# Eight zero products at the head, x^T by token halves, and the last LayerNorms dealt out anew in a two-layer decoder trunk

## The chip, the cores and the metric

The kernel runs on one core of one Trainium2 chip, in one launch. The metric is the device time of that launch in microseconds (us); lower is better. Five engines work side by side and meet through semaphores: TensorE (PE in the profile; its weight loads stand apart as PEld), VectorE (DVE), ScalarE (ACT), GpSimd (POOL) and SyncE (SP), whose part here is to issue DMAs.

## The reference

Two layers (DEPTH = 2) over 1024 tokens of width 1024 in float32. Layer 0 mixes tokens with a gated DeltaNet, layer 1 with a complex diagonal state-space layer (S5); each runs beside a 4-head cross-attention into 256 memory tokens. Cut to what matters:

```
for i in range(2):
    if i == 0:  mix, xq = gdn_mixer(x, ...)    # q, k, v, z, beta, g from one projection of x;
                                               # short conv, chunked delta rule, 8 heads
    else:       mix, xq = s5_mixer(x, ...)
    cross = memory_attention(xq, mem, w_kv[i])
    x = layer_norm(ALPHA * x + concat(mix, cross) @ w_o[i], ln1_g[i], ln1_b[i])
    x = layer_norm(ALPHA * x + square(relu(x @ w1[i])) @ w2[i], ln2_g[i], ln2_b[i])
```

`layer_norm` takes mean and variance over the 1024 channels of a token, and multiplies by (variance + 1e-5)^-1/2, a gain and a bias.

## The kernel before, in words

**Products.** Every float32 operand is split in two parts, high = the value rounded to the type fp32r (a copy on ACT) and low = the rest (a subtraction on DVE), and a product is three matmuls, high x high, high x low and low x high (`mm3`, L397 to L399). Activations are held transposed, channels on the 128 partitions and tokens in two halves of 512 (`HALF`), so a matmul has 512 columns and a projection of one block of 128 outputs takes 8 channel blocks k (`KT`) x 3 matmuls for each half.

**The first stage.** `load_xT` loads the first weight block (tile `wir`, 512 KB, split into `wih` and `wil` by `load_split`, L354, L363 and L364), the 16 gate columns (`wba`, 64 KB), then the eight 512 KB blocks of x^T (tile `x`, L981 and L983). L993 and L994 split x into `xTh` and `xTl`. Two jobs on PE eat these: `ba` (L1011 and L1012, gate columns, two matmuls for a block and half) and `wi` (first key projection, three matmuls). `gdn_consts` fills constants before that.

**The recurrence stage.** From about 205 to 695 us the delta rule runs head by head. Its chain, for each pair of 64-token chunks, is: `ks` on PE, R on DVE (L1431), `pe` on PE (L1435), a copy `e` on ACT (L1437), `pS` and `po` on PE (L1441, L1447), the new state S on DVE (L1446). Projections of the next head (`wi`, `wz`) fill PE between. DVE also works, four times, on the inverse of a triangular matrix (tile X, L1233 and L1235, 16 instructions in a row). L1335 (`mix`) and L1329 (`gb`) prepare a chunk for this chain.

**The end.** `mlp_last` computes the last two matrices of the second MLP: for each block tau of 128 tokens two PE groups (tile `tm`, 12 matmuls each), each added onto y by DVE (L938), and after a block's second group `done` calls `layer_norm`. That has two forms. In the DVE form bn_stats, bn_aggr, a scale and shift of the variance (L509 to L511) are DVE's; in the `junk` form ACT takes the sums and the squares (L502, L505) with three one-column steps on DVE between. In both forms POOL raises to the power -1/2 (L512), and DVE makes two passes over the row (L522 and L523; L514 and L517 for the last block, whose second pass and store are cut in two). In layer 1 blocks 5 and 6 take the ACT form.

**What sets the order.** The program is written in one order, and at the end `settle` reorders all of it, from `self.begin` on: it takes the written order of PE as due times, goes through a list schedule with a price for every instruction (`price`), an input being ready at `r + length + lag`, and fixes the order that results on each engine. Every engine then runs its own list strictly in order. A change of one price or of one rule can therefore move instructions far from the lines that were edited.

Of the kernel before, what the change touches and what calls it, by code (L numbers as in the profile page):

```python
# [10 lines left out]
F32 = mybir.dt.float32  # L11
F32R = mybir.dt.float32r
AF = mybir.ActivationFunctionType
ALU = mybir.AluOpType
# [15 lines left out]
def f32(ap):  # L30
    return ap.bitcast(F32)


class Trunk:
# [27 lines left out]
    def settle(self, first, last, reach=0.0, ahead=15.0, passes=1, margin=0.0, late=0.0, hold=1e3):  # L62
# [118 lines left out]
        for _ in range(passes):  # L181
# [36 lines left out]
            while len(order) < n:  # L218
# [48 lines left out]
                for y in after[x] + then[x]:  # L267
                    same = e == E.PE and ins[y].engine == e
                    ready[y] = max(ready[y], r + (0.0 if x not in deps[y] else busy if same else length + lag + (margin if ins[y].engine == E.PE else 0.0)))
# [222 lines left out]

    def layer_norm(self, y, gb, junk=None, last=None):
# [4 lines left out]
        mv = self.tile("st", [P, 4], F32, "mv")  # L498
        if junk is not None:
            s = st.rearrange("p a b -> p (a b)")  # L500
            for c in range(2):
                nc.scalar.activation(junk, halves[c], AF.Copy, accum_out=s[:, c:c + 1])  # L502
            nc.vector.tensor_scalar(mv[:, 0:1], s[:, 0:1], s[:, 1:2], -1.0 / 1024, op0=ALU.add, op1=ALU.mult)
            for c in range(2):
                nc.scalar.activation(junk, halves[c], AF.Square, bias=mv[:, 0:1], accum_out=s[:, 4 + c:5 + c])  # L505
            nc.vector.scalar_tensor_tensor(mv[:, 2:3], s[:, 4:5], s[:, 5:6], self.eps_ln, op0=ALU.add, op1=ALU.add)
        else:
            for c in range(2):
                nc.vector.bn_stats(st[:, c, :], halves[c])  # L509
            nc.vector.bn_aggr(mv[:, 0:2], st)  # L510
            nc.vector.tensor_scalar(mv[:, 2:3], mv[:, 1:2], 1024.0, 1024 * 1e-5, op0=ALU.mult, op1=ALU.add)  # L511
        nc.gpsimd.tensor_tensor(mv[:, 3:4], mv[:, 2:3], self.mhalf[:, 0:1], op=ALU.pow)  # L512
        if last is not None:
            nc.vector.scalar_tensor_tensor(y, y, mv[:, 0:1], gb[0], op0=ALU.subtract, op1=ALU.mult)  # L514
            for c in range(2):
                c = slice(c * HALF, (c + 1) * HALF)
                nc.vector.scalar_tensor_tensor(y[:, c], y[:, c], mv[:, 3:4], gb[1][:, c], op0=ALU.mult, op1=ALU.add)  # L517
                nc.sync.dma_start(last[:, c], y[:, c])
            return
        parts = [(y, slice(0, 1024))] if not isinstance(y, list) else [(y[c], slice(c * HALF, (c + 1) * HALF)) for c in range(2)]  # L520
        for o, c in parts:
            nc.vector.scalar_tensor_tensor(o, o, mv[:, 0:1], gb[0][:, c], op0=ALU.subtract if junk is None else ALU.add, op1=ALU.mult)  # L522
            nc.vector.scalar_tensor_tensor(o, o, mv[:, 3:4], gb[1][:, c], op0=ALU.mult, op1=ALU.add)  # L523
# [417 lines left out]


    def gdn_consts(self):
        nc = self.nc
# [26 lines left out]
    def load_xT(self, wba):  # L971

        nc = self.nc
        w0 = self.load_split(self.a["w_in"][8], "w1", "wi")
        nc.sync.dma_start(wba, self.a["wba"])
        self.begin = nc.cur_bb.bb.instructions[-1]
        raw = self.quad(F32, "x") + self.quad(F32, "x")
        for k in range(KT):
            if k == 0:
                for h in range(2):  # L980
                    nc.sync.dma_start(raw[0][:, h * HALF:(h + 1) * HALF], self.a["xT"][0:P, h * HALF:(h + 1) * HALF])  # L981
                continue
            nc.sync.dma_start(raw[k], self.a["xT"][k * P:(k + 1) * P])  # L983
# [4 lines left out]
        xT = self.new_xT()  # L988
        for k in range(KT):
            for h in range(2):  # L990
                s = raw[k][:, h * HALF:(h + 1) * HALF]
                hi, lo = xT[h][0][:, k, :], xT[h][1][:, k, :]
                nc.scalar.copy(hi, s)  # L993
                nc.vector.tensor_tensor(lo, s, f32(hi), op=ALU.subtract)  # L994
        return xT, w0
# [1212 lines left out]
    def run(self):  # L2208
# [131 lines left out]
    def mlp_block(self, i, B, ahead, xd, side, out, more):  # L2340
        new = []

        def done(y, tau):
            if tau == 0:
                self.gb2 = self.load_gb(self.a["ln2_g"][i:i + 1], self.a["ln2_b"][i:i + 1])
                self.nc.scalar.activation(self.gb2[0], self.gb2[0], AF.Copy, scale=32.0)
                if more:
                    new.extend(self.new_xT())
            self.layer_norm(y[tau], self.gb2, self.psum("mm", "jk") if tau in ((), (5, 6))[i] else None, last=out[tau] if tau == 7 and not more else None)
            if tau < 7 or more:  # L2350
# [96 lines left out]
```

## Time and profile before

| | us |
|---|---|
| median of 3 runs | 2511.4 (2509.89, 2511.4, 2513.75) |
| the profiled execution | 2512.02 |
| its span, first to last instruction | 2510.3 |
| PE busy in the span | 2471.1 (98%) |
| DVE busy | 1969.6 (78%) |
| ACT busy | 1283.0 (51%) |
| POOL busy | 435.9 (17%) |

DMA moves 481 MB, 192 GB/s on the mean. The mean granted TensorE clock is 0.998. PE works nearly all the time, so what counts is where it does not: the span less PE's busy time is 39 us, which the table of stretches puts at 7.9 us in the first 50, 10 us after 2490, 8.8 us between 400 and 600, and the rest in small pieces. In the profile, the column in brackets behind a row is the time for which the engine stood idle before it and what ended that.

### The profile page before, as it was taken

Reading aid. Unit: us, or ns where it says so; the run is one execution under the profiler, and the core shown is the slowest. Engines: PE = TensorE matmul, PEld = TensorE weight load, DVE = VectorE, ACT = ScalarE, POOL = GpSimd, SP = SyncE. Lnnn points to the kernel's source line nnn. Section 1 sums busy time; section 2 is a strip of 40 time slices with the busy share of each in tenths; the row PEclk is TensorE's granted clock in tenths of the full one; section 3 lists DMA queues with packets and bytes.
Section 4 is the critical chain, followed back from the end, with each engine's and each line's share of the span. In section 5 each row is a group of like instructions: output and inputs, shape, how many; then the busy total and the mean of one; then the engine's idle time right before and its main releaser. Section 6 shows DMA issues by size and latency. Waiting matters only on the chain.

```text
span 2510.3 us, 36952 instructions
## 1 busy us (share of the span) xinstructions
PE 2471.1 (98%) x12181; PEld 2063.9 (82%) x12181; DVE 1969.6 (78%) x3676; ACT 1283.0 (51%) x2730; POOL 435.9 (17%) x673
## 2 busy tenths in 40 slices
PE   8999999999999999999999999999999999999998
PEld 6888887887887887888888888888887888888886
DVE  7786888777779798879988957786687666578788
ACT  6665555554556576554444244564365555544441
POOL 1232332414002023212210123112011000000000
PEclk9999999999999999999999999999999999999999
DMA  6464585767854567487454489669736434574532
GB/s 211 119 163 125 138 257 135 237 189 226 270 166 157 192 218 236 154 297 240 148 161 134 157 245 301 214 216 331 259 131 206 155 143 164 216 255 133 168 105 97
DMA packets 320769, 481.17 MB, mean 192 GB/s; under 512 B 110225, under 2 KB 141153, under 8 KB 320577
## 3 DMA queue, kind: packets, MB, share of 16 engines
q1 hardware_dynamic: 293056, 423.76, 51.9%
q0 software_dynamic: 25216, 50.86, 6.9%
q10 hardware_dynamic: 2304, 4.20, 0.4%
q8 instruction: 96, 1.57, 0.3%
q14 instruction: 97, 0.79, 0.1%
HBM read 321.91 MB, written 156.73 MB: 191 GB/s over the span
## 4 chain that ended last, share of the span: by engine, by line
PE 87%; DVE 5%; ACT 3%; DMA 2%; issue 2%; POOL 1%; SPq 0%; DVEq 0%; POOLq 0%; ACTq 0%
PE q L398 7%; PE q L397 7%; PE q L399 7%; PE tm L397 4%; PE tm L399 4%; PE tm L398 4%; PE pA L399 3%; PE pA L397 3%; PE pA L398 3%; PE wi L397 3%; PE wi L399 3%; PE wi L398 3%; PE pC L399 2%; PE pC L397 2%; PE pC L398 2%; PE pB L397 2%
## 5 line engine op out<-in xcount | busy, mean ns | idle before, releaser
L397 PE MATMUL q<-wkh,hkh 128*128 128x512 f32 x784 | 306.2, 391 | 0.7 <-ACT G L1886 0.7
L398 PE MATMUL q<-wkl,hkh 128*128 128x512 f32 x784 | 305.9, 390 | 0.5 <-DVE wkl L901 0.5
L399 PE MATMUL q<-wkh,hkl 128*128 128x512 f32 x784 | 305.4, 390 | 0.0
L900 ACT CAST wkh<-wr 128x512 fp32r<-128x512 f32 x168 | 104.9, 624 | 237.5 <-PE q L398 186.2
L512 POOL TENSOR_TENSOR mv<-mv,mhalf 128x1 f32<-128x1 f32 x32 | 26.7, 833 | 858.9 <-DVE mv L511 634.6
L397 PEld LDWEIGHTS q<-wkh,hkh 128*128 128x128 f32 x784 | 147.2, 188 | 32.2 <-ACT G L1886 1.6
L398 PEld LDWEIGHTS q<-wkl,hkh 128*128 128x128 f32 x784 | 147.3, 188 | 31.0 <-DVE wkl L901 1.1
L399 PEld LDWEIGHTS q<-wkh,hkl 128*128 128x128 f32 x784 | 147.2, 188 | 30.5
L901 DVE TENSOR_TENSOR wkl<-wr,wkh 128x512 fp32r<-128x512 f32 x168 | 115.5, 688 | 65.8 <-issue 55.6
L397 PE MATMUL wi<-xTh,wih 128*128 128x512 f32 x384 | 159.9, 416 | 0.2 <-ACT qT L1098 0.2
L398 PE MATMUL wi<-xTl,wih 128*128 128x512 f32 x384 | 152.6, 397 | 0.0
L399 PE MATMUL wi<-xTh,wil 128*128 128x512 f32 x384 | 152.4, 397 | 0.0
L901 DVE TENSOR_TENSOR hkl<-hr,hkh 128x512 fp32r<-128x512 f32 x196 | 133.9, 683 | 0.2 <-ACT hkh L900 0.2
L900 ACT CAST hkh<-hr 128x512 fp32r<-128x512 f32 x196 | 120.8, 616 | 1.3 <-DMA hr<-hd 1.2
L397 PE MATMUL tm<-so 128*128 128x512 f32 x280 | 109.8, 397 | 0.0
L1621 ACT CAST so<-or 128x1024 fp32r<-128x1024 f32 x70 | 72.0, 1049 | 59.5 <-DMA or<-wod 42.0
L1622 DVE TENSOR_TENSOR so<-or,so 128x1024 fp32r<-128x1024 f32 x70 | 84.5, 1220 | 16.1 <-ACT so L1621 16.0
L398 PE MATMUL tm<-so 128*128 128x512 f32 x224 | 88.2, 394 | 0.0
L399 PE MATMUL tm<-so 128*128 128x512 f32 x224 | 87.4, 391 | 0.0
L399 PEld LDWEIGHTS wi<-xTh,wil 128*128 128x128 f32 x384 | 72.7, 189 | 14.8
L397 PEld LDWEIGHTS wi<-xTh,wih 128*128 128x128 f32 x384 | 73.2, 191 | 12.5 <-ACT qT L1098 0.6
L398 PEld LDWEIGHTS wi<-xTl,wih 128*128 128x128 f32 x384 | 73.2, 191 | 11.6 <-issue 0.3
(588 smaller groups left out, 7381.8 us busy)
## 6 DMA issues: line engine op xcount, KB each, us to landing
hr<-hd SPq DMA_DIRECT2D x212, 256.0 KB, 2.8
wr<-in_w_dram SPq DMA_DIRECT2D x56, 512.0 KB, 5.0
hd<-u SPq DMA_DIRECT2D x92, 256.0 KB, 2.0
w1r<-in_w_dram SPq DMA_DIRECT2D x32, 512.0 KB, 3.5
hd<-hid SPq DMA_DIRECT2D x60, 256.0 KB, 2.3
hd<-p SPq DMA_DIRECT2D x60, 256.0 KB, 2.2
w1r<-in_w_dram SPq DMA_DIRECT2D x56, 256.0 KB, 3.6
wir<-in_w_in_dram SPq DMA_DIRECT2D x24, 512.0 KB, 3.9
```

Source lines behind the costliest of these rows:

```text
L397: mm(ps, a[0], b[0], start=start, stop=False, skip_group_check=onto)
L398: mm(ps, a[0], b[1], start=False, stop=False, skip_group_check=onto)
L399: mm(ps, a[1], b[0], start=False, stop=stop, skip_group_check=onto)
L512: nc.gpsimd.tensor_tensor(mv[:, 3:4], mv[:, 2:3], self.mhalf[:, 0:1], op=ALU.pow)
L900: nc.scalar.copy(hi, s)
L901: nc.vector.tensor_tensor(lo, s, f32(hi), op=ALU.subtract)
L1621: nc.scalar.copy(hi, r)
L1622: V.tensor_tensor(lo, r, f32(hi), op=ALU.subtract)
```

## The change

It has three parts, and a fourth that follows from them.

1. **The head.** `rouse(8)` puts eight products of a zero tile with itself (128x128, float32) at PE's head; nothing reads them. `load_xT` now issues a half piece of x^T (256 KB: block 0, first 512 tokens) ahead of all, then the gate columns, then the first weight block, then all first halves of x^T, then all second halves. The first weight block is split in two steps of 512 columns.
2. **The last LayerNorms** (`end=True`, layer 1 only). The variance is no longer scaled by 1024: one DVE addition of (0, 1e-5) onto (mean, variance) takes the place of the scale and shift, and both passes wait for its result; the gain is not multiplied by 32 on ACT. Blocks 2, 3 and 4 take the ACT form in place of 5 and 6.
3. **A rule of `settle`.** For instructions written in the last 60 us of the program that are no DMA, an input from the same engine counts as ready at `busy + 0.06` in place of `length + lag`.
4. **The order.** `settle` runs over all of the changed program, and the order comes out differently in the first 60 us, in the recurrence stage, in parts of the first MLP and at the end.

```diff
-                    same = e == E.PE and ins[y].engine == e
-                    ready[y] = max(ready[y], r + (0.0 if x not in deps[y] else busy if same else length + lag + ...))
+                    same = ins[y].engine == e and (e == E.PE or not moves and spot[x] > now - 60.0)
+                    ready[y] = max(ready[y], r + (0.0 if x not in deps[y] else busy + (0.0 if e == E.PE else 0.06) if same else length + lag + ...))
...
+        elif end:
+            for c in range(2):
+                nc.vector.bn_stats(st[:, c, :], halves[c])
+            nc.vector.bn_aggr(mv[:, 4:6], st)
+            nc.vector.tensor_tensor(mv[:, 1:3], mv[:, 4:6], self.eps2, op=ALU.add)
...
+    def rouse(self, n):
+        z = self.tile("h2", [P, P], F32, "z")
+        self.nc.vector.memset(z, 0.0)
+        ps = self.psum("mm", "z", (P, P))
+        for k in range(n):
+            self.nc.tensor.matmul(ps, z, z, start=True, stop=True)
...
-        w0 = self.load_split(self.a["w_in"][8], "w1", "wi")
+        raw = self.quad(F32, "x") + self.quad(F32, "x")
+        nc.sync.dma_start(raw[0][:, 0:HALF], self.a["xT"][0:P, 0:HALF])
         nc.sync.dma_start(wba, self.a["wba"])
+        r0 = self.load_raw(self.a["w_in"][8], "wir")
...
+        for h in range(2):
+            for k in range(KT):
+                if k or h:
+                    nc.sync.dma_start(raw[k][:, h * HALF:(h + 1) * HALF], self.a["xT"][k * P:(k + 1) * P, h * HALF:(h + 1) * HALF])
...
+        self.rouse(8)
         self.gdn_consts()
...
-            self.layer_norm(y[tau], self.gb2, self.psum("mm", "jk") if tau in ((), (5, 6))[i] else None, ...)
+            self.layer_norm(y[tau], self.gb2, self.psum("mm", "jk") if tau in ((), (2, 3, 4))[i] else None, ..., end=not more)
```

**Place one, the head of the program.** SP's list before (`wir` is the weight block, `x_110` holds blocks 0 to 3 of x^T and `x_111` blocks 4 to 7):

```order
L354 DMA wir_103<-in_w_in_dram 128x1024
L975 DMA wba_102<-in_wba_dram 128x128
L981 DMA x_110<-in_xT_dram 128x512
L983 DMA x_111<-in_xT_dram 128x1024
L983 DMA x_110<-in_xT_dram 128x1024 x3
L983 DMA x_111<-in_xT_dram 128x1024 x3
```

and now (`x_114` and `x_115` are the two holders; L1056 is a 4 KB load for the gates):

```order
L992 DMA x_114<-in_xT_dram 128x512
L993 DMA wba_113<-in_wba_dram 128x128
L354 DMA wir_118<-in_w_in_dram 128x1024
L1013 DMA x_114<-in_xT_dram 128x512 x3
L1013 DMA x_115<-in_xT_dram 128x512 x3
L1056 DMA scr_90<-in_dtb_dram 128x8
L1013 DMA x_115<-in_xT_dram 128x512
```

The weight block has gone from first to third, and every piece of x^T behind it is half as large. PE's list now begins with the zero products, and both gate products of block 0 stand ahead of the first one that needs the weight block:

```order
L958 MATMUL z_81<-z_79 128x128 x8
L1038 MATMUL ba_186<-xTh_9_120,wbah_181 32x512
L1039 MATMUL ba_186<-xTl_10_121,wbah_181 16x512
L397 MATMUL wi_292<-xTh_9_120,wih_126 128x512
L398 MATMUL wi_292<-xTl_10_121,wih_126 128x512
L399 MATMUL wi_292<-xTh_9_120,wil_127 128x512
```

Before, the first five products were L1011, L397, L1012, L398 and L399.

**Place two, DVE in the recurrence stage, at the inverse that ran from 563 to 574 us.** Before (the rows on X that are left out by ending the piece here are 14 more of L1233 and L1235):

```order
L1431 SCALAR_TENSOR_TENSOR R_6176<-ks_6174,scr_79,mix_1733 128x128
L1100 SCALAR_TENSOR_TENSOR vT_6056<-cv_6057,scr_79,vT_6056 128x512 x2
L1446 SCALAR_TENSOR_TENSOR S_6234<-S_6150,scr_79,pS_6232 128x128
L1100 SCALAR_TENSOR_TENSOR vT_6056<-cv_6057,scr_79,vT_6056 128x512
L364 TENSOR_TENSOR wil_6471<-wir_6468,wih_6470 128x1024
L1233 TENSOR_TENSOR pr_5538<-X_946_5531,st_950_5577 128x512
L1233 TENSOR_TENSOR pr_951_5578<-X_946_5531,st_950_5577 128x512
```

Now (L1458 is R, L1362 is `mix`, L1356 is `gb`, L1260 the inverse):

```order
L1458 SCALAR_TENSOR_TENSOR R_6196<-ks_6194,scr_90,mix_1753 128x128
L1362 TENSOR_TENSOR mix_1753<-qk_6148,Dq_6142 128x512
L1127 SCALAR_TENSOR_TENSOR vT_6076<-cv_6077,scr_90,vT_6076 128x512
L1356 TENSOR_TENSOR gb_6144<-gb_6144,qT_5967 128x512
L1127 SCALAR_TENSOR_TENSOR vT_6076<-cv_6077,scr_90,vT_6076 128x512
L1473 SCALAR_TENSOR_TENSOR S_6254<-S_6170,scr_90,pS_6252 128x128
L1127 SCALAR_TENSOR_TENSOR vT_6076<-cv_6077,scr_90,vT_6076 128x512
L1260 TENSOR_TENSOR pr_5558<-X_948_5551,st_952_5597 128x512
```

`mix` and `gb` have moved from behind the inverse to ahead of it, and the weight split L364 from ahead of it to behind it, and behind the next R as well.

**Place three, DVE's last rows.** Before (`tm` is a PE group, `bn` and `mv` the statistics, `y_21712` the blocks 4 to 7):

```order
L522 SCALAR_TENSOR_TENSOR y_21712<-y_21712,mv_24285,gb_24047 128x1024
L938 TENSOR_TENSOR y_21712<-tm_24310,y_21712 128x512
L523 SCALAR_TENSOR_TENSOR y_21712<-y_21712,mv_24285,gb_24049 128x1024
L509 BN_STATS bn_24324<-y_21712 128x6
L510 BN_AGGR mv_24325<-bn_24324 128x2
L514 SCALAR_TENSOR_TENSOR y_21712<-y_21712,mv_24325,gb_24047 128x1024
L511 TENSOR_SCALAR mv_24325<-mv_24325 128x1
L517 SCALAR_TENSOR_TENSOR y_21712<-y_21712,mv_24325,gb_24049 128x512 x2
```

Now (L948 adds a group, L515 is the addition of (0, 1e-5), L532 and L533 the two passes, L524 and L527 those of the last block):

```order
L532 SCALAR_TENSOR_TENSOR y_21732<-y_21732,mv_24315,gb_24067 128x1024
L948 TENSOR_TENSOR y_21732<-tm_24324,y_21732 128x512
L513 BN_STATS bn_24352<-y_21732 128x6
L533 SCALAR_TENSOR_TENSOR y_21732<-y_21732,mv_24315,gb_24069 128x1024
L948 TENSOR_TENSOR y_21732<-tm_24338,y_21732 128x512
L513 BN_STATS bn_24352<-y_21732 128x6
L514 BN_AGGR mv_24353<-bn_24352 128x2
L515 TENSOR_TENSOR mv_24353<-mv_24353,eps_24071 128x2
L524 SCALAR_TENSOR_TENSOR y_21732<-y_21732,mv_24353,gb_24067 128x1024
L527 SCALAR_TENSOR_TENSOR y_21732<-y_21732,mv_24353,gb_24069 128x512 x2
```

Both passes of block 6 now stand ahead of the last addition, and the one-column step stands ahead of the last block's first pass. From the addition of block 5's second group to that of the last one, the new list has four additions, four bn_stats, two each of bn_aggr and L515, and five passes (second of block 4, both of blocks 5 and 6).

More of the change, by code (lines that the diff above doesn't have):

```diff
@@ L491, in load_gb, with layer_norm @@
         return out
-    def layer_norm(self, y, gb, junk=None, last=None):
+    def layer_norm(self, y, gb, junk=None, last=None, end=False):
         nc = self.nc
@@ L2345, in done @@
                 self.gb2 = self.load_gb(self.a["ln2_g"][i:i + 1], self.a["ln2_b"][i:i + 1])
-                self.nc.scalar.activation(self.gb2[0], self.gb2[0], AF.Copy, scale=32.0)
+                if more:
+                    self.nc.scalar.activation(self.gb2[0], self.gb2[0], AF.Copy, scale=32.0)
+                else:
+                    self.eps2 = self.tile("st", [P, 2], F32, "eps")
+                    self.nc.gpsimd.memset(self.eps2[:, 0:1], 0.0)
+                    self.nc.gpsimd.memset(self.eps2[:, 1:2], 1e-5)
                 if more:
                     new.extend(self.new_xT())
-            self.layer_norm(y[tau], self.gb2, self.psum("mm", "jk") if tau in ((), (5, 6))[i] else None, last=out[tau] if tau == 7 and not more else None)
+            self.layer_norm(y[tau], self.gb2, self.psum("mm", "jk") if tau in ((), (2, 3, 4))[i] else None, last=out[tau] if tau == 7 and not more else None, end=not more)
             if tau < 7 or more:
```

41 lines of the change are left out of this document (24 added, 17 removed).

## The prediction

> **What bounds the kernel now.** I read the page first, then the waits of PE, then the two ends in order of time.
>
> ```profile
> PE 2471.1 (98%) x12181; PEld 2063.9 (82%) x12181; DVE 1969.6 (78%) x3676; ACT 1283.0 (51%) x2730; POOL 435.9 (17%) x673
> ...
> PE 87%; DVE 5%; ACT 3%; DMA 2%; issue 2%; POOL 1%; SPq 0%; DVEq 0%; POOLq 0%; ACTq 0%
> ```
>
> ```profile
> PE ba L1011 <- ACT xTh L993: 7.9, 2, 7.2
> PE po L1432 <- ACT on L1460: 4.3, 5, 2.4
> PE pe L1435 <- DVE R L1431: 3.0, 1, 3.0
> ```
>
> PE sets the time; 2510.3 - 2471.1 = 39 us is all that it does not work. The waits (us in total, times, longest) put 7.9 us of that on the first piece of x, and the next largest on the recurrence. So the change can only win at the head, in a few stalls, and behind PE's last product. The head, in order of time:
>
> ```profile
> 0.80 0.40 SPq L354 DMA_DIRECT2D wir<-in_w_in_dram  x1
> 0.87 0.09 DVE L1091 MEMSET cv<- 128x3 f32 x2 [0.87 <-PEq L2436]
> ...
> 1.71 0.43 SPq L981 DMA_DIRECT2D x<-in_xT_dram  x1
> ...
> 4.30 1.04 ACT L363 CAST wih<-wir 128x1024 fp32r<-128x1024 f32 x1 [2.22 <-DMA wir<-in_w_in_dram]
> 5.25 0.29 ACT L1004 CAST wbah<-wba 128x128 fp32r<-128x128 f32 x1
> ...
> 6.51 0.62 ACT L993 CAST xTh<-x 128x512 fp32r<-128x512 f32 x1 [0.96 <-DMA x<-in_xT_dram]
> ...
> 7.18 0.63 PE L1011 MATMUL ba<-xTh,wbah 128*32 128x512 f32 x1 [7.18 <-ACT xTh L993]
> ...
> 7.61 0.63 PE L397 MATMUL wi<-xTh,wih 128*128 128x512 f32 x1
> ...
> 8.30 0.62 ACT L993 CAST xTh<-x 128x512 fp32r<-128x512 f32 x1 [1.17 <-DMA x<-in_xT_dram]
> ...
> 9.54 0.62 ACT L993 CAST xTh<-x 128x512 fp32r<-128x512 f32 x1 [0.62 <-DMA x<-in_xT_dram]
> ...
> 10.21 0.64 PE L1011 MATMUL ba<-xTh,wbah 128*32 128x512 f32 x1 [0.69 <-ACT xTh L993]
> ...
> 13.20 0.54 PE L1012 MATMUL ba<-xTl,wbah 128*16 128x512 f32 x1
> 13.58 0.40 PE L398 MATMUL wi<-xTl,wih 128*128 128x512 f32 x1
> ...
> 13.81 0.39 PE L399 MATMUL wi<-xTh,wil 128*128 128x512 f32 x1
> ```
>
> Three things lose time. The first product waits until 7.18. Blocks of x come 1.24 us apart (casts at 8.30 and 9.54), because each is 512 KB though the first half of it would do. And products start 0.43 us apart at first (7.18, 7.61) and 0.23 apart from 13.58 on: for 6.4 us PE runs at half speed. Thirteen products start ahead of the one at 13.58. From there PE is dense, so that point is my mark: what reaches it earlier moves all that follows.
>
> **The head.** The zero products:
>
> ```profile
> 45.91 0.89 PE kk L1159 x8
> ```
>
> These are four float32 products of 128x128 (two records each), 0.22 us apiece at full speed; eight at half speed take 8 x 0.22 x 0.43 / 0.23 = 3.3 us. The tile is zeroed first on DVE, which begins at 0.87, so they run from about 1.2 to 4.5. No real product is ready by then, as follows, so they cost nothing; were the gate columns ready at 4.2, they would cost 0.3.
>
> The loads. The weight block is now third, behind 256 and 64 KB. Its bounds: before, the third load (256 KB, the same 832 KB in all) let the cast start at 6.51, so 6.5 at the latest; alone in front it let the cast start at 4.30, and 256 KB more take 0.7 at the rate of stretch 15 to 18 below, so 5.0 at the earliest. The low rate between the two is in the other row (the last number is GB/s):
>
> ```profile
> 4.50:5.00 0.50, 0.00 (x0) 0.00 (x0) 0.00 (x0) 0.50 (x1) 0.00 (x0) 1.00 0.82 115
> 15.00:18.00 3.00, 3.00 (x15) 2.10 (x14) 1.58 (x3) 1.63 (x4) 0.00 (x0) 1.00 0.99 376
> ```
>
> I take 5.8, the middle. ACT then casts two halves of the weight block and block 1 of x, 3 x 0.62, to 7.7; block 0's five products are done by then. Eight more at 0.23 reach the mark's count at 9.5: 13.58 - 9.5 = 4.1 us gained, 4.9 and 3.4 at the ends. Splitting x^T into halves doubles the number of SP's issues (0.43 each); a half piece takes 256 KB / 376 GB/s = 0.70 us to come, so the issues stay ahead, and 0.70 is less than the 5 x 0.23 = 1.15 us of products that it feeds: no wait behind the mark. I take 0.2 off for a clock that rises a little late: **-3.9**.
>
> **The recurrence.** The order moves `mix` and `gb` ahead of the inverse and the weight split behind it.
>
> ```profile
> 561.93 1.22 DVE L364 TENSOR_TENSOR wil<-wir,wih 128x1024 fp32r<-128x1024 f32 x1
> ...
> 574.08 0.69 DVE L1335 TENSOR_TENSOR mix<-qk,Dq 128x512 f32<-128x512 f32 x1
> 574.68 0.35 DVE L1431 SCALAR_TENSOR_TENSOR R<-ks,scr,mix 128x128 f32<-128x128 f32 x1
> ...
> 575.08 0.49 PE L1435 MATMUL pe<-R,iv 128*128 128x128 f32 x2 [2.96 <-DVE R L1431]
> ```
>
> R stands behind the inverse, and PE waited 2.96 us for it. Out of R's way go the split (1.1 from start to start) and `mix` (574.08 to 574.68, 0.6); `gb`, as large, comes in (0.6). R is 1.1 us earlier. The split is then 1.1 later for the projection that needs it; that one stands behind the next R on PE too, so I charge nothing, and keep 0 as the other end. Elsewhere in this stage rows move a place or two in both directions; I take 0, with one stall like this one, more or less, as bounds (below): **-1.1**.
>
> **The tail.**
>
> ```profile
> 2493.40 1.28 DVE L522 SCALAR_TENSOR_TENSOR y<-y,mv,gb 128x1024 f32<-128x1024 f32 x1
> ...
> 2493.63 1.46 POOL L512 TENSOR_TENSOR mv<-mv,mhalf 128x1 f32<-128x1 f32 x1 [3.65 <-DVE mv L506]
> ...
> 2495.12 1.28 DVE L523 SCALAR_TENSOR_TENSOR y<-y,mv,gb 128x1024 f32<-128x1024 f32 x1 [0.44 <-POOL mv L512]
> ...
> 2499.98 0.39 PE L399 MATMUL tm<-w2h,hk 128*128 128x512 f32 x1
> ...
> 2501.14 0.69 DVE L938 TENSOR_TENSOR y<-tm,y 128x512 f32<-128x512 f32 x1
> 2501.74 1.28 DVE L523 SCALAR_TENSOR_TENSOR y<-y,mv,gb 128x1024 f32<-128x1024 f32 x1
> 2502.93 0.69 DVE L509 BATCH_NORM_STATS2 bn<-y 128x6 f32<-128x512 f32 x1
> 2503.65 0.21 DVE L510 BATCH_NORM_AGGREGATE mv<-bn 128x2 f32<-128x12 f32 x1
> 2503.90 1.28 DVE L514 SCALAR_TENSOR_TENSOR y<-y,mv,gb 128x1024 f32<-128x1024 f32 x1
> ...
> 2505.39 0.55 POOL L512 TENSOR_TENSOR mv<-mv,mhalf 128x1 f32<-128x1 f32 x1 [3.76 <-DVE mv L511]
> 2505.97 1.41 DVE L517 SCALAR_TENSOR_TENSOR y<-y,mv,gb 128x512 f32<-128x512 f32 x2 [0.73 <-POOL mv L512]
> ```
>
> PE ends at 2499.98 + 0.39 = 2500.37; the last addition starts 0.77 later, since DVE is busy with the block before, and 4.83 after it starts the final pass. Now, from that addition: 0.7 to bn_stats, 0.7 to bn_aggr, 0.25 and 0.15 to the first pass (the one-column step is between), and 1.72 from first to second pass, as from 2493.40 to 2495.12, where the power ran beside the pass too and took 1.46 in place of 0.55: 3.5. That is 1.3 less. When does the addition start? In four PE groups (4 x 12 x 0.227 = 10.9 us) DVE has four pairs of addition and bn_stats (1.35 each), four small steps (0.13 to 0.25) and five passes of 1.2: 11.9 to 12.4, that is 1.0 to 1.5 late, 0 if it comes in with 1.0 or more in hand, and 0.77 before. I take 0.9: **-1.2**, with -0.6 and -2.0 as ends.
>
> The Trainium skill, page "SBUF — State Buffer", section "SBUF: two separate sides", says that whichever of a DVE operation with two SBUF inputs and a GpSimd operation that reads SBUF starts first holds the shared ports for the whole instruction, and the other is fully blocked. By it the power starts only after the pass, an estimate of 1.28 + 0.55 = 1.8 in place of 1.72, and the step's new place, which lets the power start beside the pass, buys next to nothing. The rows agree: 1.46 beside a pass, 0.55 after one; the sum stays within 0.1 us.
>
> **The sum.** It is made against the profiled execution's own 2512.0 (span 2510.3 and 1.7 around it), which lies 0.6 above the median of the three runs: 2512.0 - 3.9 - 1.1 - 1.2 = **2505.8**. Its own range is 2503.5 to 2508, from the ends above. A measurement of this kernel can tell about 0.2% (5.0 us) from no change, so faster is below 2506.4 and slower above 2516.4; the forecast lies just beyond the first.
>
> **Rivals.** First, *the clock does not stay up*. What a pause does is shown here:
>
> ```profile
> 430.00:440.00 10.00, 6.40 (x35) 4.81 (x34) 8.16 (x18) 5.54 (x21) 9.65 (x14) 1.00 0.57 152
> 440.00:450.00 10.00, 10.00 (x57) 8.76 (x56) 8.12 (x16) 5.86 (x23) 9.05 (x17) 0.83 0.76 180
> 570.00:580.00 10.00, 6.01 (x27) 4.77 (x26) 10.00 (x17) 3.53 (x7) 4.04 (x6) 0.84 0.56 159
> ```
>
> PE was idle 3.6 us of ten, no wait longer than 2.4, and then the granted clock was 0.83: 10 x 0.17 / 0.5 = 3.4 us at half speed, a loss of 1.7. Between the zero products and block 1 PE has gaps of some 0.4 (for the gate columns), 0.9 (for the weight block) and 0.4. If these keep it at half speed, the eight products take 3.4 and not 1.8 (1.6 lost), and if until 13.5 as before, 1.2 more: 2507.4 to 2508.6, say 2508.0. For it: half speed lasted 6.4 us before, over one gap of 0.69. Against it: the work of 3.3 us ahead. The Trainium skill, page "TensorE: Matmul & The Clock Gate", section "What's actually happening", has a free-running window of about 3.4 us: one busy window lifts the clock, one idle window halves it. By that rule 3.3 us of zeros fill no whole window, and the rival would hold, while no gap under 3.4 us could halve the clock; the rows agree with the length and not with the second half, since a wait of 2.4 was enough. Chance 0.18.
>
> Second, *the new order stalls the recurrence* (the side of slower). Price of one stall as from 570 to 580: 4.0 idle and 1.7 of half speed, 5.7. One makes 2511.5, no change; two make 2517.2. It decides from the second on. For it: DVE was busy 10.00 of 10 there, and R, S and `pe` wait on its exact order; the order is new in dozens of places. Against it: the same rule made the old order, which has two such places. Chance 0.13 for one, 0.09 for two.
>
> Third, *it helps there more than one row*: both old stalls shrink below what halves the clock, 2 x 1.7 = 3.4: 2502.4. For it: 2.4 and 2.96 are single waits and one is cut already. Chance 0.12.
>
> Fourth, *the head's gain is swallowed*, the change not doing what it says: the next wait on the gates or the weights just takes the freed time, leaving 2512.0 - 2.3 = 2509.7. Against it: PE is dense from 13.58 with several projections to choose from. Chance 0.06. The forecast keeps 0.42.
>
> **Chances.** Two thirds of the forecast's own range and all of the third rival are below 2506.4, with a little of the first: 0.28 + 0.12 + 0.05 = 0.45 faster; slower is the double stall, 0.09; the rest, 0.46, is no change. The range 2501.5 to 2513 takes in the single stall and half of the third rival's spread, and leaves out the double stall and better luck.
>
> **What would show it.** Right: first `wi` product near 6.4, products 0.23 apart by 8, the 14th real product near 9.5; R some 1.1 us earlier behind that inverse, with a wait under 2; final pass about 4.4 us after PE's last product (5.6 before). Wrong: products 0.43 apart beyond 10, a granted clock below 0.9 in a stretch of 10 us that had 1.00, or the last addition over 1.5 us behind PE.

## The result and the profile after

Over 22 runs each, the kernel after took 2509.11 us in the median (2506.65 to 2517.85), the kernel before 2513.46. The ratio is 0.9984 (95% interval 0.9978 to 0.9990), so 2.5 to 5.5 us less: about 0.16%, a real gain, but inside the 0.2% that the prediction took for "no change". The forecast, 2505.8, was a gain of 6.2 us. The profiled execution of the kernel after took 2510.50 (span 2508.8), above its median, and only 1.5 us below that of before. So these two traces alone do not explain the gain, and the experiments are read by the times first.

The page of the kernel after, parts 1 and 4, and its waits on PE (us in total, times, longest):

```profile
PE 2477.6 (99%) x12197; PEld 2066.3 (82%) x12197; DVE 1973.0 (79%) x3679; ACT 1285.8 (51%) x2738; POOL 438.6 (17%) x675
...
PE 82%; DVE 6%; issue 4%; DMA 3%; POOL 2%; ACT 2%; SPq 0%; POOLq 0%; DVEq 0%; ACTq 0%
```

```profile
PE pS L1468 <- ACT e L1464: 2.0, 3, 1.3
PE pg L1911 <- DVE G1T L1860: 1.5, 1, 1.5
...
PE po L1459 <- ACT on L1487: 1.4, 4, 0.5
PE pe L1462 <- DVE R L1458: 1.2, 1, 1.2
```

PE is idle 31 us in place of 39 (3.8 of these 8 us are the zero products, which count as work). The 7.9 us for x are gone from the list, `po` has fallen from 4.3 to 1.4, R's wait from 3.0 to 1.2; the copy of `e` is now the largest (2.0, from 1.0). The head, in order of time:

```profile
1.11 3.78 PE L958 MATMUL z<-z 128*128 128x128 f32 x16 [1.11 <-DVE cv L1118]
...
3.93 0.62 ACT L1000 CAST xTh<-x 128x512 fp32r<-128x512 f32 x1 [1.86 <-DMA x<-in_xT_dram]
...
5.53 0.63 PE L1038 MATMUL ba<-xTh,wbah 128*32 128x512 f32 x1 [0.64 <-DVE wbah L1032]
...
6.30 1.14 ACT L1008 CAST wih<-wir 128x512 fp32r<-128x512 f32 x2 [1.55 <-DMA wir<-in_w_in_dram]
...
6.97 0.50 PE L397 MATMUL wi<-xTh,wih 128*128 128x512 f32 x1 [0.48 <-ACT wih L1008]
...
8.67 0.42 PE L1038 MATMUL ba<-xTh,wbah 128*32 128x512 f32 x1 [0.47 <-ACT xTh L1000]
...
10.78 0.40 PE L397 MATMUL wi<-xTh,wih 128*128 128x512 f32 x1
```

The last row is the 14th real product: 2.80 us earlier than before (13.58), where 4.1 was forecast. How far is PE ahead later? Two products that stand in the same place of both orders tell it: the first `sc` of the cross-attention and the first transpose behind layer 0. Their rows in the time order of the kernel before:

```profile
80.61 0.28 PE L397 MATMUL sc<-kv,qh 128*128 128x256 f32 x1
...
733.29 0.60 PE L530 MATMUL xt<-ident,y 128*128 128x128 f32 x4
```

and of the kernel after:

```profile
78.64 0.28 PE L397 MATMUL sc<-kv,qh 128*128 128x256 f32 x1
...
730.14 0.60 PE L540 MATMUL xt<-ident,y 128*128 128x128 f32 x4
```

The lead is 2.80 at the mark, 1.97 at 80 us, 3.15 at 733 us. PE's last product ends at 2499.06, before at 2500.37: 1.31 is left. The end of the kernel after:

```profile
2498.67 0.39 PE L399 MATMUL tm<-w2h,hk 128*128 128x512 f32 x1
...
2499.58 1.27 DVE L533 SCALAR_TENSOR_TENSOR y<-y,mv,gb 128x1024 f32<-128x1024 f32 x1
2500.77 0.68 DVE L948 TENSOR_TENSOR y<-tm,y 128x512 f32<-128x512 f32 x1
...
2502.65 1.28 DVE L524 SCALAR_TENSOR_TENSOR y<-y,mv,gb 128x1024 f32<-128x1024 f32 x1
2502.76 1.58 POOL L521 TENSOR_TENSOR mv<-mv,mhalf 128x1 f32<-128x1 f32 x1 [4.02 <-DVE mv L515]
2504.38 1.42 DVE L527 SCALAR_TENSOR_TENSOR y<-y,mv,gb 128x512 f32<-128x512 f32 x2 [0.44 <-POOL mv L521]
```

The chain from the last addition to the final pass is 3.61, as forecast (3.5; 4.83 before). But the addition starts 1.71 behind PE's end, since block 6's second pass (2499.58) stands ahead of it. The final pass is 5.32 after PE's end, 5.60 before: 0.28 gained, not 1.2.

### The profile page after: what moved, and what is told of

It is laid out like the page before. It is cut to its first block, busy times and chain, and to the rows that moved or that the text cites. A ratio compares the mean times of both kernels' runs of the same rounds, so it can differ in the third digit from the quotient of the medians.

```text
span 2508.8 us, 37028 instructions
## 1 busy us (share of the span) xinstructions
PE 2477.6 (99%) x12197; PEld 2066.3 (82%) x12197; DVE 1973.0 (79%) x3679; ACT 1285.8 (51%) x2738; POOL 438.6 (17%) x675
## 4 chain that ended last, share of the span: by engine, by line
PE 82%; DVE 6%; issue 4%; DMA 3%; POOL 2%; ACT 2%; SPq 0%; POOLq 0%; DVEq 0%; ACTq 0%
PE q L398 7%; PE q L397 7%; PE q L399 7%; PE pA L399 4%; PE pA L397 4%; PE pA L398 4%; PE tm L397 4%; PE tm L398 4%; PE tm L399 4%; PE wi L397 2%; PE wi L399 2%; PE wi L398 2%; PE pC L399 2%; PE pC L397 2%; PE pC L398 2%
## 5 line engine op out<-in xcount | busy, mean ns | idle before, releaser
L397 PE MATMUL q<-wkh,hkh 128*128 128x512 f32 x784 | 306.5, 391 | 0.6 <-ACT G L1913 0.6
L398 PE MATMUL q<-wkl,hkh 128*128 128x512 f32 x784 | 305.8, 390 | 0.5 <-DVE wkl L911 0.5
L399 PE MATMUL q<-wkh,hkl 128*128 128x512 f32 x784 | 305.3, 390 | 0.0
L397 PEld LDWEIGHTS q<-wkh,hkh 128*128 128x128 f32 x784 | 147.2, 188 | 32.1 <-ACT G L1913 1.4
L398 PEld LDWEIGHTS q<-wkl,hkh 128*128 128x128 f32 x784 | 147.2, 188 | 30.8 <-DVE wkl L911 1.1
L399 PEld LDWEIGHTS q<-wkh,hkl 128*128 128x128 f32 x784 | 147.2, 188 | 30.6
L397 PE MATMUL wi<-xTh,wih 128*128 128x512 f32 x384 | 159.4, 415 | 0.6 <-ACT wih L1008 0.5
L399 PE MATMUL wi<-xTh,wil 128*128 128x512 f32 x384 | 152.2, 396 | 0.0
L398 PE MATMUL wi<-xTl,wih 128*128 128x512 f32 x384 | 151.8, 395 | 0.0
L397 PE MATMUL tm<-so 128*128 128x512 f32 x280 | 110.4, 398 | 0.2 <-ACT so L1648 0.2
L399 PE MATMUL tm<-so 128*128 128x512 f32 x224 | 87.9, 393 | 0.0
L398 PE MATMUL tm<-so 128*128 128x512 f32 x224 | 87.7, 392 | 0.0
L399 PEld LDWEIGHTS wi<-xTh,wil 128*128 128x128 f32 x384 | 72.2, 188 | 15.3 <-DVE wil L1009 0.4
L397 PEld LDWEIGHTS wi<-xTh,wih 128*128 128x128 f32 x384 | 72.7, 189 | 13.2 <-ACT wih L1008 1.3
L398 PEld LDWEIGHTS wi<-xTl,wih 128*128 128x128 f32 x384 | 72.7, 189 | 11.6
```

The costliest lines, as they stand in the source:

```text
L397: mm(ps, a[0], b[0], start=start, stop=False, skip_group_check=onto)
L398: mm(ps, a[0], b[1], start=False, stop=False, skip_group_check=onto)
L399: mm(ps, a[1], b[0], start=False, stop=stop, skip_group_check=onto)
```

## The experiments

The first four split the change; the next two separate the head from the order that comes with it; the rest test causes. All were timed beside the kernel before, whose median was 2512.73 us beside one to four, 2513.77 beside five to eight, 2512.90 beside nine to eleven and 2513.59 beside twelve. Behind each median stands the ratio to the kernel before, with its 95% interval. "Lead" is how much earlier than in the kernel before PE reaches a place. Line numbers are each kernel's own.

**One: the head alone.** The kernel before, with `load_xT` and `rouse` as in the change.

```
+        self.rouse(8)
         self.gdn_consts()
...
-        w0 = self.load_split(self.a["w_in"][8], "w1", "wi")
+        raw = self.quad(F32, "x") + self.quad(F32, "x")
+        nc.sync.dma_start(raw[0][:, 0:HALF], self.a["xT"][0:P, 0:HALF])
...
```

> The kernel before with the head of the change alone: zero products, half pieces of x^T, weight block third. The list of PE is that of the kernel after throughout, the recurrence's new order included; the last LayerNorms are the old ones. Theory 1 (the head makes the gain, the tail next to nothing): 14th real product at about 10.8 us as in the kernel after, final pass about 5.6 us after PE's last product, and 3.5 to 4.3 us below the kernel before. Rival 1 (the new LayerNorms make the gain): no more than 1 us below the kernel before. Rival 2 (the new order of the recurrence makes it, the head's gain being swallowed later): the same time as theory 1, but PE's lead over the kernel before, followed from instruction to instruction, falls to 0 between 15 and 200 us and comes back between 400 and 700.

2508.09 us; 0.9981 (0.9973 to 0.9990). All of the gain is there. The trace contradicts the reason, though: the 14th product at 12.25, a lead of 0.29 at 80 us, and 4.23 at 733. So in this run next to nothing of the head's gain was left at 80 us, and the recurrence brought the rest. (The trace has no half speed in the recurrence, the kernel before's has 6.8 us; that is part of it.) The windows of the head show why the mark came late (us, PE's busy time, ..., granted clock, DMA share, GB/s):

```profile
5.92:9.33 3.41, 1.99 (x6) 0.70 (x5) 1.85 (x4) 2.44 (x5) 0.00 (x0) 1.00 0.97 350
9.33:12.74 3.41, 3.04 (x9) 1.66 (x9) 3.41 (x7) 3.16 (x6) 0.00 (x0) 0.50 1.00 333
```

The clock had come up at 5.9. PE then waited 1.4 us for the weight block and was back at half speed from 9.33 to 12.74.

**Two: the tail alone.** The kernel after with the old head, `load_xT` as before and no `rouse`.

```
-        self.rouse(8)
...
+        w0 = self.load_split(self.a["w_in"][8], "w1", "wi")
         nc.sync.dma_start(wba, self.a["wba"])
...
```

> The kernel after with the head of the kernel before: what is left of the change is the new LayerNorms of the second layer's end and the rule for the last 60 us. The lists of PE are those of the kernel before, and DVE's differ in the last 5% alone. Theory 1: PE's last product as in the kernel before, the final pass 5.3 us after it (5.6 before), so 0.2 to 0.4 us faster, which the timing can't tell from nothing. The prediction's step (1.2 us) would show the final pass 4.4 us after it. Rival 1 (the tail makes the gain): 3 us or more faster.

2512.46 us; 0.9995 (0.9986 to 1.0004). PE's last product ends at 2502.28, the final pass is at 2507.42, 5.14 behind:

```profile
2501.89 0.39 PE L399 MATMUL tm<-w2h,hk 128*128 128x512 f32 x1
...
2507.42 1.41 DVE L527 SCALAR_TENSOR_TENSOR y<-y,mv,gb 128x512 f32<-128x512 f32 x2 [0.44 <-POOL mv L521]
```

So by the traces the LayerNorms give 0.3 to 0.5 us, which the time can't tell from nothing. More than half of the tail's term was never there.

**Three: no zero products.**

```
-        self.rouse(8)
```

> The kernel after without the eight zero products; all lists are otherwise the same. Theory 1 (the zero products raise the clock while the loads come in): the clock rises only when a stretch full of real products has gone by, after 9.5 us, products 0.43 apart until then, 14th real product at 11.6 to 13.0 in place of 10.8, and 0.8 to 2.4 us above the kernel after. Rival (the clock would be up by then anyway, the earlier loads make all of the head's gain): 14th real product at 10.8, the time of the kernel after.

2509.48 us; 0.9985 (0.9976 to 0.9994). In the trace products stay 0.43 apart until 12.9, the 14th comes at 12.02 (inside 11.6 to 13.0), and the lead at 80 us is -0.14. By the time it can't be told from the kernel after. Again a kernel without any lead at 80 us is some 3 us faster than the kernel before.

**Four: blocks 5 and 6 on ACT.**

```
-... if tau in ((), (2, 3, 4))[i] ...
+... if tau in ((), (5, 6))[i] ...
```

> The kernel after with blocks 5 and 6 of the last LayerNorm on ScalarE as in the kernel before, in place of 2, 3 and 4; nothing else moves outside the last 60 us. Theory 1 (VectorE has too much to do in the last four groups of PE, because blocks 5 and 6 have come to it; that is what put the last addition 1.7 us behind PE's last product): the last addition 0.1 to 0.8 behind, the final pass 4.0 to 4.9 after PE's last product (5.3 in the kernel after), 0.4 to 1.3 us faster than the kernel after. Rival (the last addition is late because it waits for PE's result or its store, wherever the blocks are normalised): no change against the kernel after.

2509.35 us; 0.9985 (0.9976 to 0.9993).

```profile
2497.09 0.39 PE L399 MATMUL tm<-w2h,hk 128*128 128x512 f32 x1
...
2498.86 0.68 DVE L948 TENSOR_TENSOR y<-tm,y 128x512 f32<-128x512 f32 x1
...
2500.63 1.28 DVE L533 SCALAR_TENSOR_TENSOR y<-y,mv,gb 128x1024 f32<-128x1024 f32 x1
...
2503.21 1.41 DVE L527 SCALAR_TENSOR_TENSOR y<-y,mv,gb 128x512 f32<-128x512 f32 x2
```

Theory 1 missed. The addition is 1.38 behind, and the final pass 5.73, later than in the kernel after (5.32). Whichever blocks DVE is spared, block 6's two passes still fall into the last microseconds. What counts is their place in DVE's list.

**Five and six: head and order apart.** The order on every engine comes from the list schedule over the whole program, so a new head also reorders the recurrence. Here it is replaced by a fixed list: from 90 us of PE work on, one kernel has the new head and the old kernel's order, the other the old head and the order that the new head led to.

```
-        order = best[1]
+        order = pinned()
```

> The head of the change (zero products, half pieces, weight block third), but from 90 us of PE work on the order on all engines is pinned to that of the kernel before; the LayerNorms are the old ones. Theory 1 (the prediction's: what the head gains is passed on): 2.5 to 4 us below the kernel before, as the head alone with its own order was. Theory 2 (formed on the runs so far: of the head's lead 0 to 2 us is left at 80 us, and the rest of the gain is the new order of the recurrence): 0.3 to 2 us below the kernel before.

> The kernel before, loads and all, but from 90 us of PE work on the order on all engines is pinned to the one that the changed head led to. Theory 1: 0 to 1.1 us below the kernel before (1.1 being the prediction's term for R). Theory 2: 1.5 to 3.5 us below it, PE's lead 0 at 80 us and 1.5 to 4 at 700 us.

New head, old order: 2512.20 us; 0.9992 (0.9983 to 1.0001). Old head, new order: 2509.44 us; 0.9981 (0.9972 to 0.9989). That speaks for theory 2, though kernel six gained more than its 1.5 to 3.5 us. The order alone is worth as much as the whole change (2.8 to 7.0 us, against 2.5 to 5.5). The head alone is worth 2.0 (from 4.3 faster to 0.3 slower), which can't be told from nothing; the two intervals overlap a little. All experiments say the same: two and five, with the old order, have 0.9995 and 0.9992, and every kernel with the new one has 0.9985 or less, whatever its head. The recurrence stage as one stretch (length, then PE's busy time), in the kernel before:

```profile
200.00:700.00 500.00, 489.04 (x2744) 416.60 (x2743) 394.62 (x784) 258.00 (x790) 138.62 (x219) 0.99 0.66 196
```

after:

```profile
200.00:700.00 500.00, 492.79 (x2749) 418.85 (x2748) 397.23 (x787) 261.85 (x800) 141.29 (x220) 0.99 0.66 197
```

new head with the old order:

```profile
200.00:700.00 500.00, 489.73 (x2746) 417.24 (x2746) 394.09 (x785) 259.90 (x796) 139.18 (x220) 0.99 0.64 197
```

old head with the new order:

```profile
200.00:700.00 500.00, 492.43 (x2751) 417.68 (x2750) 396.26 (x786) 260.55 (x796) 140.78 (x219) 0.99 0.65 197
```

Idle there is 500 less busy: 11.0 and 10.3 us with the old order (11.2 in experiment two), 7.2 and 7.6 with the new one (8.2 and 7.7 in one and three). About 3 us less, whatever the head. Half speed hides idle time, since PE then works longer on the same products. So here is the same with half of the half-speed time added, an estimate of the work lost in it: 13.7 to 16.4 us in the three profiles with the old order, 8.2 to 13.1 in the seven with the new (the kernel after, one, three, four, six, seven, eight). The order still gains. At the first landmark (80 us) kernel six is 0.32 behind the kernel before, at the second (733 us) 1.18 ahead, less than the 1.5 to 4 that theory 2 expected.

**Seven: the weight block in two loads.** The first 256 KB go behind the gate columns, the rest behind two half pieces of x; from 90 us on the order is pinned to the kernel after's.

```
-        r0 = self.load_raw(self.a["w_in"][8], "wir")
+        r0 = self.tile("raw", [P, 1024], F32, "wir")
+        nc.sync.dma_start(r0[:, 0:HALF], self.a["w_in"][8][:, 0:HALF])
+        for k in range(1, 3):
+            nc.sync.dma_start(raw[k][:, 0:HALF], self.a["xT"][k * P:(k + 1) * P, 0:HALF])
+        nc.sync.dma_start(r0[:, HALF:], self.a["w_in"][8][:, HALF:])
```

> The kernel after with the first weight block loaded in two pieces of 256 KB: the first right behind the gate columns, the second behind two half pieces of x^T; from 90 us on the order is pinned to that of the kernel after. Theory (the first product of wi and the next blocks of x wait for bytes that they don't need yet): half pieces of x cast from 6.5 on in place of 7.4 to 8.0, 14th real product at 9.5 to 10.8 (10.8 to 12.3 in the kernel after and its kin), 0.5 to 1.5 us below the kernel after. Rival (what limits is the clock, which falls back for one window of 3.4 us in two of three such heads): the loads earlier, the 14th product still at 11 to 12, the time of the kernel after within 0.5 us.

2509.36 us; 0.9980 (0.9971 to 0.9990). The 14th product came at 11.86. PE waited 2.07 us in one piece instead of several short ones (a pair of x pieces is cast at 7.08, not 6.5), and the clock was at half from 7.4 to 10.8. The lead at 80 us was 1.42, within what the other heads gave (0.29 to 1.97). The rival holds. It is in keeping with this that what comes first matters less than whether PE is kept busy.

**Eight: four more zero products** where PE waits for the weight block.

```
+        z, ps = self.z
+        for k in range(4):
+            nc.tensor.matmul(ps, z, z, start=True, stop=True)
```

> The kernel after with four more zero products between the gate products of block 0 and the first product of wi, where PE waits 0.5 to 1.4 us for the weight block; all else in the same order. Theory (that wait is what lets the clock fall back): full clock from 6 us on without a break, products 0.23 apart, 14th real product at 10 to 10.8, 0.5 to 1.5 us below the kernel after. Rival (the clock falls back for another reason, or the fall costs nothing later): half speed from about 9.3 to 12.8 again, the time of the kernel after within 0.5 us.

2507.44 us; 0.9970 (0.9959 to 0.9982), over six runs. By the ratios that is 3.5 us better than the kernel after, by the medians against the kernel before beside each 2.0. The intervals just overlap.

```profile
5.48 0.63 PE L1051 MATMUL ba<-xTl,wbah 128*16 128x512 f32 x1
5.90 1.44 PE L1016 MATMUL z<-z 128*128 128x128 f32 x8
7.17 0.49 PE L405 MATMUL wi<-xTh,wih 128*128 128x512 f32 x1
```

The gap is filled, the clock stays up, the 14th product starts at 10.95 (10 to 10.8 expected, 10.78 in the kernel after), the lead at 80 us is 1.78. Of the five profiles with eight zero products alone (the kernel after, one, four, five, seven) four fell back to half speed for 3.41 us in the head. Of the five with twelve (eight to twelve) none did. That filling the gap keeps the clock up is thus shown for the head. What it is worth in time is not: the lead is no larger than the kernel after's 1.97, and the recurrence scatters by more.

**Nine to twelve: the stalls themselves.** All are kernel eight with instructions moved by hand in the pinned list. At 433 us (nine), POOL's power for the output's norm goes ahead of three DMA issues, the copy `e` ahead of a weight cast on ACT, S ahead of a weight split on DVE, and `ks` with three products ahead of `po` on PE. At 571 us (ten), R goes ahead of the last reductions of X, and `e`, S, `vT` and `gb` go forward. Eleven has both, and at the end block 6's second pass behind the last block's variance step. Twelve is nine with that last edit. As lists, the moves on one engine at each place:

```
POOL at 433 us          DVE at 571 us             DVE at the end
 ntd   (DMA issue)       pr   (X)                 -y    block 6, second pass
+scr   (power)          +R                         y    last addition
 ntd   (DMA issue)       X    reduction            bn, mv, mv
 ntd   (DMA issue)       X    reduction           +y    block 6, second pass
 ntd   (DMA issue)      -R                         y    last block, first pass
-scr   (power)
```

> The kernel with the four more zero products, its order pinned, and one spot of the order edited, the stall near 433 us: the power of the output's norm goes ahead of three DMA issues on GpSimd, the copy of e, th and vT and the four scalings (on) ahead of a weight cast on ScalarE, the new state S ahead of a weight split on VectorE, and ks with three wz products ahead of po on PE. Theory (PE's idle time there comes from who stands behind whom, and it is what halves the clock afterwards): waits at pS and po below 0.6 each (1.3 and 0.5 to 0.7 before), no half speed after 436 us in most runs (6.83 us of it before), 2.5 to 5 us below the kernel with the four more zero products. Rival (the recurrence's chain is simply that long, and what is saved here is waited for a few us later, at R or at the weight that is now cast later): less than 1 us.

2505.88 us; 0.9973 (0.9963 to 0.9982). The stretch from 430 to 450 us in kernel eight:

```profile
430.00:450.00 20.00, 16.89 (x86) 14.08 (x85) 16.06 (x33) 11.15 (x42) 17.04 (x28) 0.83 0.75 201
```

and in kernel nine, with its wait at `pS` from the time order below it:

```profile
430.00:450.00 20.00, 18.33 (x105) 15.52 (x104) 17.61 (x37) 12.47 (x45) 16.39 (x27) 0.91 0.73 194
```

```profile
433.10 0.49 PE L1480 MATMUL pS<-e,kdl 128*128 128x128 f32 x2 [0.37 <-ACT e L1476]
```

Idle fell from 3.1 to 1.7 us, the wait at `pS` from 1.3 to 0.37, the wait at `po` went, and one half-speed window is left of two. So these two waits come from who stands behind whom. That the stall as a whole does is not shown: here, too, half speed hides idle time. Two later kernels have the full clock all through this stretch. Ten, with the old places at this spot, and below it twelve, with the new ones and its largest wait:

```profile
430.00:450.00 20.00, 16.67 (x104) 14.16 (x103) 17.66 (x38) 12.46 (x45) 17.22 (x29) 1.00 0.72 202
```

```profile
430.00:450.00 20.00, 16.82 (x107) 14.29 (x105) 18.00 (x40) 12.15 (x45) 17.45 (x28) 1.00 0.71 189
```

```profile
439.84 1.16 PE L1373 MATMUL qk<-qT,kT 128*128 128x128 f32 x8 [1.69 <-ACT jk L1360]
```

PE idles 3.3 us in ten, as in one (3.3), and 3.2 in twelve: what is saved at `pS` and `po` is waited for at `qk`, behind the weight cast that was put later on ACT. That is the rival. The time of nine is 1.6 us below kernel eight's median, but the ratios (0.9973 and 0.9970) don't tell the two apart.

> The same kernel with the four more zero products, edited at the stall near 571 us alone: R goes ahead of the last reductions of the inverse X on VectorE, e ahead of the copy of X on ScalarE, S, vT and gb ahead of oT, the next R ahead of mix and a weight split. Theory: the wait of 1.2 us at pe is gone, some 1 us less idle between 570 and 580, half speed there in fewer runs: 0.7 to 2.5 us below the kernel with the four more zero products. Rival (PE then waits for vT or for the next R instead): less than 0.5 us.

2508.82 us; 0.9982 (0.9973 to 0.9991): no gain, the rival holds. Its profile has no half speed in the whole recurrence, as the theory had hoped, and five of its eleven runs have a mean clock of 0.999 (none of kernel eight's six has); the median is no better for it. R's wait of 1.2 is gone, and in its place:

```profile
570.77 0.66 PE L1382 MATMUL vt<-ident,vT 128*128 128x128 f32 x4 [0.82 <-DVE vT L1142]
...
571.99 0.50 PE L405 MATMUL wi<-xTh,wih 128*128 128x512 f32 x1 [0.56 <-ACT zc L1395]
```

> Both edits of the recurrence's order, and at the end the second pass of block 6 behind the last block's variance step in place of ahead of the last addition, on the kernel with the four more zero products. Theory: the sum of both, and the final pass 4.8 to 5.0 us after PE's last product (5.3 before): 3.5 to 7.5 us below the kernel with the four more zero products, the fastest of all. Rival (the stalls move on): within 1.5 us of it.

2506.43 us; 0.9977 (0.9968 to 0.9986): within the rival's 1.5 us of kernel eight, not the sum.

> The kernel after with the four more zero products, the edit of the stall near 433 us, and the second pass of block 6 behind the last block's variance step; the order near 571 us as in the kernel after. Theory: the parts that held in the runs before add up: 6.5 to 8.5 us below the kernel before (ratio 0.9966 to 0.9974), PE idle 1.5 to 2.0 us between 430 and 450 us, the final pass 4.9 to 5.1 us after PE's last product. Rival (the idle time saved near 433 us is lost again by what the half-speed windows do afterwards): 4 to 5 us below it, as the kernel after.

2506.59 us; 0.9972 (0.9961 to 0.9984), 7.0 us below the kernel before. The time is in the theory's range, the reason is not: PE's idle time from 430 to 450 was 3.2, not 1.5 to 2.0, as shown above. The tail's edit held in both, a little better than expected in this one:

```profile
2495.14 0.39 PE L407 MATMUL tm<-w2h,hk 128*128 128x512 f32 x1
...
2495.88 0.67 DVE L956 TENSOR_TENSOR y<-tm,y 128x512 f32<-128x512 f32 x1
...
2500.21 1.41 DVE L535 SCALAR_TENSOR_TENSOR y<-y,mv,gb 128x512 f32<-128x512 f32 x2
```

The addition is 0.35 behind PE's end (2495.53), the final pass 4.68 (5.03 in eleven; 5.1 to 5.5 in the kernel after, two, three and seven to ten, which have the tail without this edit). Kernels eight, nine and twelve beat the kernel before by 0.27 to 0.30%, and can't be told from each other.

## Why the prediction was right, and where it was not

The range held the time, and "no change" (0.46, against 0.45 for faster) came true. That says little for the working, since the range is 11.5 us wide and the 2512.0 that the sum starts from lies in it. The point was 3.3 us too low; as a gain, 6.2 us was forecast and 4.0 measured, for the kernel before came out at 2513.46 and not at 2512.0. The working behind it fails in all three terms: two were too large, one too small. That their sum came this near is luck.

**The head, 3.9.** The mark came 2.8 us earlier in the kernel after's profile, 1.3 to 2.0 in those of one, four and five. Two steps failed. "I take 5.8" for the weight block's cast: it was 6.30, and 6.3 to 6.8 in one, four and five, the late half of the bounds given (5.0 to 6.5) or beyond; behind it block 1 was cast at 8.00, not at about 7.0. And "I take 0.2 off for a clock that rises a little late": it rose early (at 6.2 in the kernel after), but in four profiles of five it did not stay, which is the first rival. The kernel after's own profile was the fifth. Of what was left, another 0.8 to 1.4 went between 14 and 80 us. Part of it is one wait for a weight split:

```profile
57.45 0.50 PE L398 MATMUL mv<-wvl,memh 128*128 128x512 f32 x1 [0.29 <-DVE wvl L377]
```

"From there PE is dense, so that point is my mark: what reaches it earlier moves all that follows" was thus wrong too, and the fourth rival (the head's gain is swallowed) deserved far more than 0.06: with the order held, the head is worth 2.0 us (0.3 slower to 4.3 faster).

**The recurrence, 1.1.** The direction was right, the size was not: R's wait fell from 2.96 to 1.21, by 1.75 where 1.1 was worked out. "Elsewhere in this stage rows move a place or two in both directions; I take 0" was the step that failed. Idle from 200 to 700 fell from 11.0 to 7.2 us, and the order alone is worth 2.8 to 7.0 us. The stretch around R's stall, before and after:

```profile
560.00:590.00 30.00, 26.01 (x129) 21.66 (x128) 25.31 (x44) 10.40 (x29) 12.26 (x20) 0.94 0.55 153
```

```profile
560.00:590.00 30.00, 28.07 (x133) 22.90 (x132) 25.39 (x43) 10.29 (x26) 16.03 (x27) 0.94 0.68 194
```

So 2.1 of these 3.8 us are here. The rest is in small pieces: 0.7 between 450 and 560, 0.7 from 430 to 450 and 0.6 behind 590, and 0.3 more idle ahead of 430. `po` waits far less than before (4.3 to 1.4), but at the same spot `pS` waits longer. I had costed the row that I could follow and set all others to nothing. The second rival (the new order stalls) was wrong in its sign. The third (both old stalls shrink) was right in direction, but in the kernel after's profile they did not shrink below what halves the clock; in kernel one's they did.

**The tail, 1.2.** The chain was right (3.61 for 3.5), the start was not: "I take 0.9" against a count that gave 1.0 to 1.5, and 1.71 came. The order list shows block 6's second pass ahead of the last addition; reading that row would have given its 1.2 us. The "wrong if" of 1.5 was met, and so was the one on the clock: 430 to 440 had 1.00 before and is at half speed from 436.33 in the kernel after. On the ports the Trainium skill ("SBUF — State Buffer", "SBUF: two separate sides") and the trace agree again: the power took 1.58 beside the pass, 0.55 alone before, and the final pass began 1.73 after the first.

## What to carry to other kernels

Where one list schedule orders the whole program, an edit's price has two parts: what it does where it stands, and the new order far away. Hold the order fixed and run both halves before believing either. A gain at the head counts only when it is still there at a later landmark, so follow PE's lead from place to place. A wait just long enough to halve the clock costs more than it shows. Filler products in it kept the clock up where moving loads about did not; what that is worth in time is not shown here. And compare idle times only at the same clock, for half speed fills idle time with slow work.

## What the hardware showed

Half speed comes in whole windows: stretches of 3.41 or 6.83 us, on a grid of 3.41 us that lies differently in every run (the two in the profile of before begin at 440.18 and 576.72, 40.0 windows apart). What it goes with here is PE's busy time in the window ahead. The windows around the first, in the kernel before:

```profile
433.36:436.77 3.41, 2.17 (x10) 1.53 (x9) 3.38 (x7) 1.88 (x5) 3.40 (x6) 1.00 0.52 126
436.77:440.18 3.41, 1.05 (x7) 0.64 (x6) 1.42 (x3) 1.83 (x7) 3.39 (x6) 1.00 0.34 93
440.18:443.60 3.42, 3.42 (x13) 2.94 (x12) 2.92 (x7) 2.28 (x10) 3.42 (x7) 0.50 0.69 160
```

and in the kernel after:

```profile
432.92:436.33 3.41, 1.48 (x8) 1.02 (x7) 3.31 (x6) 2.50 (x6) 3.40 (x6) 1.00 0.33 55
436.33:439.75 3.42, 2.89 (x10) 1.98 (x9) 2.30 (x5) 3.05 (x14) 3.42 (x8) 0.50 0.68 188
439.75:443.16 3.41, 3.41 (x16) 3.22 (x15) 2.30 (x8) 1.63 (x5) 3.41 (x7) 0.50 0.78 202
```

2.17 us of work in a window kept the clock; 1.05 and 1.48 lost it, for one window or two. Over the fourteen profiles, all 13 full-speed windows with at most 1.6 us of PE work were followed by half speed, none with 2.17 or more was, and between the two it went both ways (11 of 23 halved). From half speed, 2.8 to 3.1 us of work went both ways too, and 3.13 or more always led back to full speed. So one stall can cost 0, 1.7 or 3.4 us of PE's work beside the wait, by where the grid falls on it. That is in keeping with kernel one, which had no half-speed window in the recurrence while the kernel after had three windows' worth with the same order. How much it explains of the 3.6 to 8.0 us by which runs of one kernel differ (11.2 in the kernel after) is not shown. In kernel ten the five runs with a mean clock of 0.999 are on average 1.9 us faster than the five with 0.997, where 5.0 would be due if all the half-speed time were lost work; and kernel eight's six runs, all at 0.997, lie up to 4.1 us apart. The Trainium skill ("TensorE: Matmul & The Clock Gate", "What's actually happening") gives the window's length, and the trace agrees; an idle window, as it has it, was not needed.

Also unexpected: in the first microseconds the profile's clock column reads 1.00 until the first change is recorded (the kernel without zero products has 1.00 from 9 to 13 us with products 0.43 apart). There the pitch of the products tells the clock, not the column.
